# Sums and high parts ahead of a product's evacuation, low parts behind it, in a Strassen feed-forward

## The chip, the cores and the metric

The kernel runs on one core of a Trainium2 chip. The metric is device time of one execution in microseconds: 1438.63 us is the median of three runs (1437.92 to 1440.17). A single profiled execution took 1436.92 us, of which the trace covers a span of 1435.1 us from the first instruction to the last. All durations below come from that execution.

## What is computed

A decoder block over a sequence of 1024 positions and 1024 channels, in float32: adaLN-modulated RMS norm, a differential attention branch and a causal convolution branch with sigmoid gates, an output projection, and then a feed-forward part, which is what the change touches:

```
h2 = rmsnorm(x, norm2_g) * (1 + sc2) + sh2
fg, fu = split(h2 @ w_ffn_in)            # 1024 -> 2 x 2816
x = x + gt2 * ((silu(fg) * fu) @ w_ffn_out)   # 2816 -> 1024
return rmsnorm(x, final_g)
```

The 2816 hidden channels are 22 tiles of 128 (the gated tiles, numbered 0 to 21). Activations lie transposed: channels on partitions, positions along the free dimension.

## The kernel before

**Precision.** Every float32 matrix product is made of three matmuls. An operand is split into a high part (ScalarE, called ACT, writes a rounded copy, `split_hi`) and a low part (VectorE, called DVE, subtracts the high part from the source). The three matmuls are high by high, high by low, low by high.

**Strassen form.** Both halves of the feed-forward use a seven-product form of a 2 x 2 block product. A `Pair` (line 1150) covers two gated tiles of the gate matrix or of the up matrix: pair i works on tiles 2(i//2) and 2(i//2)+1, even i on the gate, odd i on the up side. There are 22 pairs of seven products, each product twelve matmuls of 128 x 512 (four blocks of the contraction, three matmuls each). The products of a pair go to three PSUM banks, X, Z, X, Z, X, Y, X (line 1152), so that the next product but one adds into the same bank. In between, `evacuate(p)` reads the bank out: after products 0, 1, 2 ACT copies it to `kepta`, `keptc`, `keptb`; after products 3, 4, 5 DVE adds the kept copy and ACT applies SiLU (gate), or DVE adds and multiplies with the gate (up); after product 6 one of them reads the bank. TensorE may add to a bank only when it has been read out.

**Weights.** `load` fetches the raw weights of pair i+2 at product 1 of pair i. `prepare` makes a weight block for a product: for some a DVE sum of raw blocks (`tt`), then the ACT high part, then the DVE low part. Blocks are made `LEAD` = 6 products ahead, in a turn of ten: six tiles `wb` and four `wbp`.

**Staging of the second half.** The gated tiles of nine up pairs (tiles 0 to 17) are the left operands of the output product, again in Strassen form. `g_steps` (line 1299) makes for each two tiles seven blocks (four of them with a DVE sum, all with an ACT high part and a DVE low part) and stores them to DRAM from GpSimd's queue (`gs_d`). The seven steps run one in a product, from product 4 of the up pair to product 3 of the next gate pair; for the first tiles two in a product. Tiles 18 to 21 are stored as they are (`g_d`), and are used at the end in the common form (three matmuls each, no sums).

**The output product.** `Group` (line 1267) covers two of the eight output tiles and three pairs of gated tiles: twelve groups of seven products of nine matmuls. Its blocks come back from `gs_d` (`gb`, GpSimd's queue). Its evacuation adds the bank on DVE to the residual tile `x1r`, which is loaded from DRAM on SP's queue (line 1474). Last come the four common tiles: their weights are loaded (line 1540) and their products added (from line 1570), then the final norm.

**Order.** In this stage TensorE, DVE and ACT issue in the program's order (`in_order`, line 1399), so one late instruction holds all behind it on its engine. The queues of SP and GpSimd have no such written order; the framework places their DMAs, and buffers are taken from shared pools: 32 slots of 128 x 1024 (`slot`), the `wb` pool of six, and small pools. The main loop is at line 1479; for each product it runs, in this order:

```
prepare(nprep)         # up to two: sum, high part, low part
g.product(p)           # TensorE
late.pop(0)()          # a staging step: sum, high, low, store
g.evacuate(p)
```

Of the kernel before, what the change touches and what calls it, by code (L numbers as in the profile page):

```python
# [10 lines left out]
F32 = mybir.dt.float32  # L11
F32R = mybir.dt.float32r
AF = mybir.ActivationFunctionType
ALU = mybir.AluOpType
AX = mybir.AxisListType

P = 128
S = 1024
D = 1024
KD = D // P  # L20
# [6 lines left out]
NFF = DFF // P  # L27
# [3 lines left out]
HB = 512  # L31
# [39 lines left out]
NWB = 10  # L71
LEAD = 6
LEAD2 = 4
NST = 9
GP = 3

GB = ("A11", "S1", "S2", "S4", "S3", "A12", "A22")
# [21 lines left out]
def tile_hybrid_block(ctx: ExitStack, tc: tile.TileContext, xT, vecs, cvec, lamv, relb, bsel, bmask, jrev,  # L99
                      w_ada, w_v, w_in, w_oa, w_oc, w_out, w_fi, w_fo, outT):  # L100
    nc = tc.nc
# [25 lines left out]
    V, A, T, G = Engine(nc.vector), Engine(nc.scalar), Engine(nc.tensor), nc.gpsimd  # L127
# [11 lines left out]
    def slot(name, dt=F32):  # L139
        return sp.tile([P, S], dt, tag="s4", name=name)  # L140

    def t2(name, dt=F32):
        return tp.tile([P, HB], dt, tag="t2", name=name)
# [10 lines left out]
    def hf_sl(hf):  # L154
        return slice(hf * HB, (hf + 1) * HB)

    def split_hi(dst, src, scale=1.0):
        return A.activation(dst, src, AF.Copy, scale=scale)

    def split(hi, lo, src):  # L160
        split_hi(hi, src)
        V.tensor_tensor(out=lo, in0=src, in1=hi.bitcast(F32), op=ALU.subtract)
# [7 lines left out]
    class Weights:  # L170
# [4 lines left out]
        def load(self):  # L175
            self.raw = wp.tile([P, D], F32, tag="wraw", name=f"wr_{self.name}")
            if len(self.src.shape) == 3:
                k = self.src.shape[0]
                nc.sync.dma_start(self.raw[:, :self.n].rearrange("p (a n) -> p a n", a=k),
                                  self.src.rearrange("a p n -> p a n"))  # L180
            else:
                nc.sync.dma_start(self.raw[:, :self.n], self.src)
# [19 lines left out]
    def mm3(out, sh, sl, mh, ml, start, stop, **kw):  # L202
        T.matmul(out, sh, mh, start=start, stop=False, **kw)
        T.matmul(out, sh, ml, start=False, stop=False, **kw)
        T.matmul(out, sl, mh, start=False, stop=stop, **kw)
# [114 lines left out]
    y = []  # L320
# [40 lines left out]
    def bankG(name):  # L361
        return psG.tile([P, HB], F32, tag="G", name=name)

    with tc.tile_pool(name="psS", bufs=2, space=bass.MemoryType.PSUM) as psS, \
# [253 lines left out]
        class Proj:  # L618
# [5 lines left out]
            def step(self, s):  # L624
                hf, k = divmod(s, KD)
                if s == 0:
                    self.out = self.begin()
                if k == 0:
                    self.ps = bankG("proj")
                ks = slice(k * P, (k + 1) * P)  # L630
                mm3(self.ps, self.w.hi[:, ks], self.w.lo[:, ks], hhi[k][:, hf_sl(hf)], hlo[k][:, hf_sl(hf)],
                    k == 0, k == KD - 1)
                if k == KD - 1:
                    self.evac(self.ps, self.out, hf)
# [185 lines left out]
        for h in range(H):  # L820
# [8 lines left out]
            sm, wf, tw, nm = {}, {}, {}, {}  # L829
# [63 lines left out]
    with tc.tile_pool(name="ps2", bufs=6, space=bass.MemoryType.PSUM) as ps2, ExitStack() as fxs:  # L893
# [112 lines left out]
        for m in range(0, KD, 2):  # L1006
            i = [j[1] for j in jobs].index(m + 1) + 1
# [29 lines left out]
        x1 = []  # L1037
# [59 lines left out]
        g_d = dp.tile([NFF, P, S], F32, name="g_d")  # L1097
        gs_d = dp.tile([NST * 7, P, S], F32R, name="gs_d")
        acts = {}
        fx, ada_last = [], []  # L1100
# [49 lines left out]
        class Pair:  # L1150
# [4 lines left out]
            n = HB  # L1155
# [34 lines left out]
            def prepare(self, p):  # L1190
                self.low(self.high(p))
# [69 lines left out]

            def store(self, n):
                f = self.f + n
                if self.up and f >= 2 * NST:
                    G.dma_start(g_d[f], hidden[f])

        class Group(Pair):

            n = GP * P
# [9 lines left out]
            def load(self):  # L1279
                b = []  # L1280
                for n in range(2):
                    raw = self.raw(self.up)
                    c0 = self.g * 2 * self.n
                    nc.sync.dma_start(raw[:, :2 * self.n], w_fo[self.m + n][:, c0:c0 + 2 * self.n])
                    t = raw[:, :2 * self.n].rearrange("p (a h n) -> p h a n", h=2, n=P)
                    b.append((t[:, 0], t[:, 1]))
                (b11, b21), (b12, b22) = b
                self.b = dict(B11=b11, B21=b21, B12=b12, B22=b22)
# [10 lines left out]
        def g_steps(i):  # L1299

            a11, a21 = (hidden[2 * i][:, hf_sl(hf)] for hf in range(2))
            a12, a22 = (hidden[2 * i + 1][:, hf_sl(hf)] for hf in range(2))

            def put(name, src):
                t = slot("gst", F32R)
                split(t[:, :HB], t[:, HB:], src)
                G.dma_start(gs_d[i * 7 + GB.index(name)], t)  # L1307

            def summed(name, out, x, y, op=ALU.subtract):
                def f():  # L1310
                    t = out if out is not None else t2("gs1")
                    V.tensor_tensor(out=t, in0=x, in1=y, op=op)
                    put(name, t)
                return f

            return [lambda: put("A12", a12), lambda: put("A22", a22), lambda: put("A11", a11),
                    summed("S1", None, a21, a22, ALU.add), summed("S3", a21, a11, a21), summed("S2", a11, a22, a21),
                    summed("S4", a12, a12, a11)]

        hidden = {}  # L1320
        pairs = [Pair(i) for i in range(NFF)]
# [1 line left out]
        order = [(pairs[j], p) for p in (0, 5, 1, 2, 3, 4, 6) for j in range(2)]  # L1323
        order += [(g, p) for g in pairs[2:] for p in range(7)]
        nblock, nfx = [0], [NWB - 4]
# [126 lines left out]
        nprep = 17  # L1452

        gacts = {}
        x1 = []
        ORDER = [a for a, b, x in Pair.PRODUCTS]
        wanted = [(g, name, k) for g in range(NST // GP) for name in ORDER for k in range(GP)]

# [13 lines left out]
        def x1r():  # L1472
            x1.append(slot(f"x1r{len(x1)}"))
            nc.sync.dma_start(x1[-1], x1_d[len(x1) - 1])

        seq = pairs + [Group(i) for i in range(NST // GP * KD // 2)]
        order += [(g, p) for g in seq[NFF:] for p in range(7)]
        late = g_steps(0)
        for n, (g, p) in enumerate(order):
            if n < 14:  # L1480
                continue
            i = n // 7
            first = i < NFF
            if p == (1 if first else 3) and i + 2 < len(seq):
                seq[i + 2].load()
            for _ in range(2):
                if nprep < len(order) and nprep <= n + (LEAD if nprep < 7 * NFF else LEAD2):
                    nfx[0] = NWB - 4 if nprep < 7 * NFF else 2
                    prepare(nprep)
                    nprep += 1  # L1490
            g.product(p)
            if first:
                if g.up and p == 4 and g.i // 2 < NST:
                    late = g_steps(g.i // 2)
                for _ in range(2 if n < 18 else 1):
                    if late:
                        late.pop(0)()
            g.evacuate(p)
            if first:
                if not g.up and p == 5 and ada_todo and g.i >= 4:  # L1500
                    (c, k), ch = ada_todo.pop(0), slot("ada2")
                    nc.sync.dma_start(ch, w_ada[c, k])
                    ada_last.append((c, k, ch))
                if g.up and p == 2 and ada_last:
                    ada_sum(*ada_last.pop(0))
                if i == NFF - 1:
                    fetch_blocks(0, GP)
                    if p >= 5:
                        x1r()
            else:  # L1510
                if i < NFF + 4 and len(x1) < KD:
                    x1r()
                if g.m == 2 and p == 0:
                    fetch_blocks(g.g + 1, 7)
                elif g.m == KD - 2:
                    fetch_blocks(g.g + 1, GP)
# [10 lines left out]
            split(hi, raw, raw.bitcast(F32))  # L1527
            return hi, raw

        grp = list(range(2 * NST, NFF))  # L1530
        n = len(grp)
        raws = [fetch(f) for f in grp]
        g_acts = [g_split(f, raw) for f, raw in zip(grp, raws)]
# [1 line left out]
        for q in range(0, KD, S // (n * P)):  # L1535
            nm = S // (n * P)
            lo = slot("fol", F32R)
            hi = slot("foh", F32R)
            raw = wp.tile([P, D], F32, tag="wraw", name="for")
            nc.sync.dma_start(raw.rearrange("p (m c) -> p m c", m=nm),  # L1540
                              w_fo[q:q + nm, :, grp[0] * P:(grp[0] + n) * P].rearrange("m p c -> p m c"))
            split(hi, lo, raw)
            for i in range(nm):
                wl.append((hi[:, i * n * P:(i + 1) * n * P], lo[:, i * n * P:(i + 1) * n * P]))

        parts = (slice(0, HB), slice(HB, HB + HB // 2), slice(HB + HB // 2, S))
        stf, accs, lasts, rest = {}, {}, {}, []
# [22 lines left out]
        for i, hs in enumerate(parts):  # L1570
# [3 lines left out]
            for m in range(KD):  # L1574
# [4 lines left out]
                t = x1[m][:, hs]  # L1579
# [83 lines left out]
```

## Time and profile before

| | |
|---|---|
| median of three runs | 1438.63 us |
| profiled execution | 1436.92 us |
| its span | 1435.1 us |
| TensorE matmul busy (PE) | 1350.5 us, 94% |
| weight loads of TensorE (PEld) | 1094.1 us, 76% |
| VectorE (DVE) | 1070.8 us, 75% |
| ScalarE (ACT) | 637.7 us, 44% |
| GpSimd (POOL) | 104.1 us, 7% |
| mean granted clock of TensorE | 0.985 of full |

Busy shares are means over stages with different limits. The feed-forward pairs run from about 710 us to 1191 us of the span, the output product's groups to 1374, the common tiles and the final norm to the end. Matmuls are pipelined and their ends are modelled, so the distance between the starts of two products is the safer measure than a busy share. An engine named as the releaser of a wait is the one that came last by the profile.

### The profile page before, as it was taken

What the parts mean: (1) busy time and instruction counts of PE and PEld (TensorE: products, weight loads), DVE (VectorE), ACT (ScalarE), POOL (GpSimd) and SP (SyncE); (2) the same over time, 40 slices, a digit from 0 to 9 for tenths busy, and PEclk for the clock granted to TensorE, in tenths of its full rate; (3) what the DMA queues carried; (4) which work ended last, traced back from release to release, by engine and by line L of the source; (5) the groups of instructions that cost most, each with busy time, mean ns of one, the idle gap of its engine ahead of it and who ended that gap; (6) DMA issues with size and microseconds to landing.
All of it is one profiled execution on the core that took longest, in us unless ns stands there. A gap on an engine that the chain in (4) does not pass through costs nothing. (4 is left out here: it accounts for less than half of the span.)

```text
span 1435.1 us, 16435 instructions
## 1 busy us (share of the span) xinstructions
PE 1350.5 (94%) x6070; PEld 1094.1 (76%) x6070; DVE 1070.8 (75%) x1698; ACT 637.7 (44%) x1079; POOL 104.1 (7%) x181
## 2 busy tenths in 40 slices
PE   7999999999999999999987999999999997999996
PEld 5778787877888887788765777777777786888886
DVE  7837698899988996976896666666766645777775
ACT  5536766666412117433764444444444431222255
POOL 0000000000000000000001000011000022112004
PEclk9999999999999999999999999999999998999998
DMA  8511011000111124278313443453443359587313
GB/s 312 168 35 40 30 30 30 30 30 31 45 53 50 44 89 132 88 262 309 103 59 123 141 146 125 154 175 134 153 152 136 132 198 385 192 302 264 110 30 118
DMA packets 57811, 184.43 MB, mean 129 GB/s; under 512 B 6361, under 2 KB 9345, under 8 KB 57730
## 3 DMA queue, kind: packets, MB, share of 16 engines
q1 hardware_dynamic: 37154, 110.49, 23.2%
q0 software_dynamic: 20000, 72.36, 14.0%
q8 instruction: 48, 0.79, 0.2%
q10 hardware_dynamic: 576, 0.52, 0.1%
q14 instruction: 33, 0.27, 0.1%
HBM read 139.83 MB, written 43.52 MB: 128 GB/s over the span
## 5 line engine op out<-in xcount | busy, mean ns | idle before, releaser
L112 DVE SCALAR_TENSOR_TENSOR cacc<-u,vec,cacc 128x1022 f32<-128x1022 f32 (+28 forms) x87 | 110.2, 1267 | 2.2
L112 PE MATMUL proj<-hhi,wh_in 128*128 128x512 f32 x239 | 99.3, 415 | 1.7 <-DVE kl L124 1.7
L112 ACT ACTIVATE wbp<-tt 128x512 fp32r<-128x512 f32 (+1 forms) x66 | 38.1, 579 | 131.3 <-DVE tt L112 110.8
L112 PE MATMUL proj<-hhi,wl_in 128*128 128x512 f32 x240 | 94.9, 395 | 0.0
L112 PE MATMUL proj<-hlo,wh_in 128*128 128x512 f32 x240 | 94.7, 394 | 0.0
L112 PE MATMUL fx<-A,wb 128*128 128x512 f32 x335 | 80.1, 393 | 13.0 <-DVE g L112 13.0
L112 PE MATMUL fx<-S,wb 128*128 128x512 f32 x312 | 76.6, 394 | 8.9 <-ACT keptb L112 5.0
L112 PEld LDWEIGHTS fx<-A,wb 128*128 128x128 f32 x335 | 62.3, 188 | 29.2 <-DVE g L112 12.7
L112 ACT ACTIVATE wb<-tt 128x512 fp32r<-128x512 f32 (+1 forms) x68 | 41.1, 606 | 94.3 <-DVE tt L112 77.9
L112 DVE TENSOR_TENSOR wb<-tt,wb 128x512 fp32r<-128x512 f32 (+1 forms) x68 | 44.7, 660 | 48.0 <-ACT wb L112 47.9
L112 PE MATMUL fz<-S,wb 128*128 128x512 f32 x312 | 76.1, 392 | 1.7 <-DVE S L112 1.6
L112 DVE TENSOR_TENSOR wbp<-tt,wbp 128x512 fp32r<-128x512 f32 (+1 forms) x66 | 41.3, 627 | 48.1 <-ACT wbp L112 48.1
L112 PEld LDWEIGHTS fx<-S,wb 128*128 128x128 f32 x312 | 57.7, 188 | 25.6 <-ACT keptb L112 7.1
L112 PEld LDWEIGHTS fz<-S,wb 128*128 128x128 f32 x312 | 58.0, 188 | 16.6 <-DVE S L112 2.4
L112 PE MATMUL fx<-gb,wbp 128*128 128x512 f32 x282 | 68.6, 390 | 0.1
L112 ACT ACTIVATE gst<-g 128x512 fp32r<-128x512 f32 x54 | 33.9, 629 | 69.1 <-DVE g L112 42.9
L112 PE MATMUL fx<-S,wbp 128*128 128x512 f32 x216 | 53.8, 396 | 8.2 <-ACT keptb L112 4.6
L112 PEld LDWEIGHTS fx<-gb,wbp 128*128 128x128 f32 x282 | 52.8, 188 | 11.5 <-DMA gb<-gs_d 0.5
L1307 POOL DMA_DIRECT2D gs_d<-gst x63 | 33.5, 532 | 382.5 <-DVE gst L112 382.5
L112 PE MATMUL fz<-S,wbp 128*128 128x512 f32 x216 | 55.2, 406 | 6.4 <-ACT keptc L112 4.9
L124 ACT ACTIVATE e<-sc,mn 128x512 f32<-128x512 f32 (+7 forms) x64 | 47.1, 739 | 25.9 <-DVE mn L124 25.0
L112 PEld LDWEIGHTS fx<-S,wbp 128*128 128x128 f32 x216 | 39.7, 188 | 21.4 <-ACT keptb L112 6.6
(347 smaller groups left out, 3610.4 us busy)
## 6 DMA issues: line engine op xcount, KB each, us to landing
gs_d<-gst POOLq DMA_DIRECT2D x63, 512.0 KB, 2.9
gb<-gs_d POOLq DMA_DIRECT2D x59, 512.0 KB, 9.4
ada<-in_w_ada SPq DMA_DIRECT2D x32, 512.0 KB, 4.3
rawu<-in_w_fi SPq DMA_DIRECT2D x22, 512.0 KB, 3.5
rawg<-in_w_fi SPq DMA_DIRECT2D x22, 512.0 KB, 3.6
adac<-in_w_ada SPq DMA_DIRECT2D x16, 512.0 KB, 5.3
wr_wo<-in_w_out SPq DMA_DIRECT2D x16, 512.0 KB, 5.0
wr_in<-in_w_in SPq DMA_DIRECT2D x15, 512.0 KB, 3.5
```

Of the source, the lines that this page charges most:

```text
L112: self.last = f(*args, **kw)
L124: self.last = self.chain(f, *args, **kw) if self.chain else f(*args, **kw)
L1307: G.dma_start(gs_d[i * 7 + GB.index(name)], t)
```

## The change

In the main loop the weight block and the staging step are cut in two: the sum and the high part are issued between a product and its evacuation, the low parts (and the staging block's store) behind the evacuation. One staging step runs in a product, never two. The lead is five products, and the turn of weight blocks eight (four `wb`, four `wbp`). Of the seven staging blocks of two tiles, three still take a slot and four take a tile of the `wb` pool. The Strassen form covers tiles 2 to 19; tiles 0, 1, 20 and 21 are in the common form, so that their weights are no longer contiguous and are loaded in two halves. The residual tiles are fetched at products 3 and 5 of the first groups (two in a group) instead of one in each product.

```diff
-NST = 9
+STR = range(1, 10)
+NST = len(STR)
...
-                if self.up and f >= 2 * NST:
+                if self.up and f // 2 not in STR:
                     G.dma_start(g_d[f], hidden[f])
...
-            def put(name, src):
-                t = slot("gst", F32R)
-                split(t[:, :HB], t[:, HB:], src)
-                G.dma_start(gs_d[i * 7 + GB.index(name)], t)
...
+            def step(name, src, x=None, y=None, op=ALU.subtract):
+
                 def f():
-                    t = out if out is not None else t2("gs1")
-                    V.tensor_tensor(out=t, in0=x, in1=y, op=op)
-                    put(name, t)
+                    t = src
+                    if x is not None:
+                        t = src if src is not None else t2("gs1")
+                        V.tensor_tensor(out=t, in0=x, in1=y, op=op)
+                    if name in ("A11", "S1", "S4"):
+                        b = slot("gst", F32R)
+                    else:
+                        b = fx[0].tile([P, D], F32R, tag="wb", name="gstw", bufs=NWB - 4)
+                    split_hi(b[:, :HB], t)
+
+                    def rest():
+                        V.tensor_tensor(out=b[:, HB:], in0=t, in1=b[:, :HB].bitcast(F32), op=ALU.subtract)
+                        G.dma_start(gs_d[(i - STR[0]) * 7 + GB.index(name)], b)
+                    return rest
                 return f
...
-        late = g_steps(0)
+        late = []
...
+            g.product(p)
+            if first and g.up and p == 4 and g.i // 2 in STR:
+                late = g_steps(g.i // 2)
+            lows = []
             for _ in range(2):
-                if nprep < len(order) and nprep <= n + (LEAD if nprep < 7 * NFF else LEAD2):
-                    nfx[0] = NWB - 4 if nprep < 7 * NFF else 2
-                    prepare(nprep)
+                if nprep < len(order) and nprep <= n + (LEAD if n < 16 else LEAD - 1 if nprep < 7 * NFF else LEAD2):
+                    nfx[0] = NWB - 6 if nprep < 7 * NFF else 2
+                    h = order[nprep][0]
+                    lows.append(partial(h.low, h.high(order[nprep][1])))
                     nprep += 1
-            g.product(p)
-            if first:
-                if g.up and p == 4 and g.i // 2 < NST:
-                    late = g_steps(g.i // 2)
-                for _ in range(2 if n < 18 else 1):
-                    if late:
-                        late.pop(0)()
+            if late:
+                lows.append(late.pop(0)())
             g.evacuate(p)
+            for f in lows:
+                f()
...
-                if i < NFF + 4 and len(x1) < KD:
+                if p in (3, 5) and len(x1) < KD:
                     x1r()
...
-        grp = list(range(2 * NST, NFF))
+        grp = [f for f in range(NFF) if f // 2 not in STR]
...
-            nc.sync.dma_start(raw.rearrange("p (m c) -> p m c", m=nm),
-                              w_fo[q:q + nm, :, grp[0] * P:(grp[0] + n) * P].rearrange("m p c -> p m c"))
+            for i in range(0, n, 2):
+                nc.sync.dma_start(raw.rearrange("p (m c) -> p m c", m=nm)[:, :, i * P:(i + 2) * P],
+                                  w_fo[q:q + nm, :, grp[i] * P:(grp[i] + 2) * P].rearrange("m p c -> p m c"))
```

## Rows read from the trace of the kernel before

**Rows 1.** The page: busy time, share of the span and instructions of each engine.
```profile
PE 1350.5 (94%) x6070; PEld 1094.1 (76%) x6070; DVE 1070.8 (75%) x1698; ACT 637.7 (44%) x1079; POOL 104.1 (7%) x181
```

**Rows 2.** Windows: length, busy us (instructions) by engine, granted clock, DMA share, GB/s.
```profile
765.00:796.00 31.00, 22.05 (x83) 16.59 (x82) 19.16 (x30) 13.45 (x24) 3.72 (x7) 0.89 0.49 170
...
924.00:966.00 42.00, 38.78 (x168) 30.80 (x167) 29.06 (x45) 17.47 (x32) 3.72 (x7) 1.00 0.44 150
...
1136.00:1191.00 55.00, 55.00 (x244) 45.56 (x243) 30.17 (x47) 18.14 (x32) 10.95 (x21) 1.00 0.55 185
1191.00:1214.00 23.00, 14.73 (x55) 11.65 (x54) 8.83 (x15) 2.64 (x6) 6.17 (x12) 0.78 1.07 389
```

**Rows 3.** Waits of TensorE, 764 to 1191: us in total, times, longest.
```profile
PE fx L112 <- DVE g L112: 15.3, 9, 1.7
PE fx L112 <- ACT keptb L112: 9.6, 9, 1.6
```

**Rows 4.** Timeline of TensorE, late pairs: start, us, instruction, [idle before <-releaser].
```profile
985.41 2.88 PE L112 MATMUL fz<-S,wb 128*128 128x512 f32 x12
988.77 3.01 PE L112 MATMUL fx<-S,wbp 128*128 128x512 f32 x12 [0.49 <-ACT kepta L112]
...
995.85 3.04 PE L112 MATMUL fx<-S,wbp 128*128 128x512 f32 x12 [1.01 <-ACT keptb L112]
...
1003.29 5.73 PE L112 MATMUL fx<-A,wb 128*128 128x512 f32 x24 [1.69 <-DVE g L112]
...
1136.46 2.88 PE L112 MATMUL fz<-S,wb 128*128 128x512 f32 x12
...
1190.86 2.20 PE L112 MATMUL fx<-gb,wbp 128*128 128x512 f32 x9
```

**Rows 5.** Timeline of TensorE, first gate pair.
```profile
764.61 2.88 PE L112 MATMUL fz<-S,wb 128*128 128x512 f32 x12
...
776.17 5.49 PE L112 MATMUL fz<-S,wbp 128*128 128x512 f32 x12 [4.86 <-ACT keptc L112]
...
796.26 2.88 PE L112 MATMUL fz<-S,wb 128*128 128x512 f32 x12
```

**Rows 6.** Timeline, a gate pair with staging: sums, low part, high part, read-out.
```profile
819.79 0.69 DVE L112 TENSOR_TENSOR g<-g 128x512 f32<-128x512 f32 x1
...
823.22 0.69 DVE L112 TENSOR_TENSOR wbp<-tt,wbp 128x512 fp32r<-128x512 f32 x1 [0.70 <-ACT wbp L112]
823.83 0.69 DVE L112 TENSOR_TENSOR g<-g,g 128x512 f32<-128x512 f32 x1
824.60 0.63 ACT L112 ACTIVATE gst<-g 128x512 fp32r<-128x512 f32 x1 [1.41 <-DVE g L112]
825.13 0.58 ACT L112 ACTIVATE keptb<-fx 128x512 f32<-128x512 f32 x1
```

**Rows 7.** Timeline at the change from pairs to groups.
```profile
1192.66 2.56 SPq L1474 DMA_DIRECT2D x1r<-x_d  x5
...
1202.51 0.75 DVE L112 SCALAR_TENSOR_TENSOR x1r<-fx,cols,x1r 128x512 f32<-128x512 f32 x1 [9.14 <-DMA x1r<-x_d]
...
1203.37 4.18 PE L112 MATMUL fx<-gb,wb 128*128 128x512 f32 x9 [8.27 <-issue]
...
1210.03 2.20 PE L112 MATMUL fx<-gb,wbp 128*128 128x512 f32 x9
```

**Rows 8.** The page: DMA issues, KB each, median us from issue to landing.
```profile
gs_d<-gst POOLq DMA_DIRECT2D x63, 512.0 KB, 2.9
```

**Rows 9.** Timeline at the start of the common tiles.
```profile
1373.94 0.39 PE L124 MATMUL fo<-gh,foh 128*128 128x512 f32 x1
...
1377.53 1.22 DVE L124 TENSOR_TENSOR fol<-for,foh 128x1024 fp32r<-128x1024 f32 x1
```

**Rows 10.** The tile x1r, 1185 to 1215: its loads to their landing.
```profile
DMA to landing us min/median/max: 11.7/13.6/15.7
```

**Rows 11.** Timeline of the first gate pair, ACT.
```profile
775.00 0.63 ACT L112 ACTIVATE gst<-gs 128x512 fp32r<-128x512 f32 x1 [3.08 <-DMA gs_d<-gst]
```

More of the change, by code (lines that the diff above doesn't have):

```diff
@@ L1282, in load @@
                     raw = self.raw(self.up)
-                    c0 = self.g * 2 * self.n
+                    c0 = 2 * P * STR[0] + self.g * 2 * self.n
                     nc.sync.dma_start(raw[:, :2 * self.n], w_fo[self.m + n][:, c0:c0 + 2 * self.n])
@@ L1302, in g_steps @@
             a12, a22 = (hidden[2 * i + 1][:, hf_sl(hf)] for hf in range(2))
-            def put(name, src):
-                t = slot("gst", F32R)
-                split(t[:, :HB], t[:, HB:], src)
-                G.dma_start(gs_d[i * 7 + GB.index(name)], t)
-            def summed(name, out, x, y, op=ALU.subtract):
-                def f():
-                    t = out if out is not None else t2("gs1")
-                    V.tensor_tensor(out=t, in0=x, in1=y, op=op)
-                    put(name, t)
-                return f
-            return [lambda: put("A12", a12), lambda: put("A22", a22), lambda: put("A11", a11),
-                    summed("S1", None, a21, a22, ALU.add), summed("S3", a21, a11, a21), summed("S2", a11, a22, a21),
-                    summed("S4", a12, a12, a11)]
+            def step(name, src, x=None, y=None, op=ALU.subtract):
+                def f():
+                    t = src
[11 more added lines that the diff above has]
+                    return rest
+                return f
+            return [step("A12", a12), step("A22", a22), step("A11", a11), step("S1", None, a21, a22, ALU.add),
+                    step("S3", a21, a11, a21), step("S2", a11, a22, a21), step("S4", a12, a12, a11)]
         hidden = {}
```

## The prediction

> **What bounds the kernel now.** I read the page first: TensorE has 1350.5 us of matmul in a span of 1435.1, DVE 1070.8, ScalarE (ACT) 637.7 [rows 1]. TensorE sets the time, so a change pays only where TensorE stands still. The windows say where that is. Through the steady part of the gated feed-forward (924 to 966 us) it is busy 38.78 of 42 us at full clock; from 1136 to 1191, with no staging steps left, 55.00 of 55; at the change to the output product (1191 to 1214) 14.73 of 23, at a granted clock of 0.78; in the first stretch (765 to 796) 22.05 of 31 at 0.89 [rows 2]. The waits of the feed-forward name one cause: TensorE waits for a PSUM bank to be read out, by DVE (15.3 us, nine times) or by ACT's copy keptb (9.6 us, nine times) [rows 3]. DMA and weights hardly appear there.
>
> The TensorE timeline gives the size. A product without a wait takes 2.72 us: the twenty from 1136.46 to 1190.86 take 54.40 [rows 4]. A period is one gate pair and one up pair, fourteen products, 38.08 us. The eight periods from 796.26 to 1136.46 take 340.20, so 42.53 each: 4.45 lost in each, 35.6 in all [rows 4, 5]. Inside a period the loss lies in the gate pair: 985.41 to 988.77 is 3.36 (0.64 too long), the next two products 7.08 (1.64), the next two 7.44 (2.00) [rows 4]. The first gate pair, with two staging steps in a product, takes 31.65 from 764.61 to 796.26 where seven products want 19.04: 12.6 lost, 4.86 of it in one wait for the copy keptc, after which twelve matmuls took 5.49 [rows 5]. Together 48.2 us.
>
> Why the read-out is late shows in ACT's and DVE's order. Each product's queue holds sum, high part (ACT), low part (DVE) of a weight block, the same three of a staging step, and only then the read-out. Every low part waits for its high part, so the two engines take turns: one staging sum starts at 819.79, the next at 823.83, 4.04 us apart against 2.72 of a product, and keptb comes at 825.13 behind the second step's high part of 824.60 [rows 6]. DVE is busy only 29.06 of 42 us there and ACT 17.47 [rows 2]: it is the order, not the amount.
>
> **The change, part by part.** *Low parts behind the read-out.* Per product DVE now holds weight sum, staging sum, (read-out), weight low, staging low; ACT holds weight high, staging high, read-out. Let TensorE end a product at E, with ACT's copy (0.58 us) as read-out [rows 6]. The copy is done near E+0.8; the bank's next writer starts at E+2.72, one product later, so 1.9 us are spare. ACT then makes the next product's two high parts (0.63 each, 0.53 apart as from 824.60 to 825.13) [rows 6] by E+2.0; their sums were issued ahead and are done. DVE's two lows (0.69, and 0.61 apart as from 823.22 to 823.83) [rows 6] end at E+2.75, its next two sums at E+3.4 and E+4.0, and the next highs are due at E+3.5 and E+4.05. So a product with everything in it holds 2.72. The tightest is the gate pair's fourth, where five DVE instructions fall together (two sums, the bank's read-out, two lows): 5 x 0.61 = 3.05, 0.33 over; the next has three (1.83) and pays it back. Work is unchanged: 29.06 us of DVE against 38.08 of a period.
>
> So the 35.6 us and the 12.6 us go. The first gate pair has no staging at all now, since the first two tiles leave the Strassen form. The last gate pair gets seven steps instead: 4.45 in the old order, nothing in the new by the same schedule. Bounds: nothing gained (0) to all 48.2. I take 1.5 back, 0.15 for each of ten gate pairs, for the tight fourth product: 46.7.
>
> *Lead of five, eight weight blocks in turn, four of seven staging blocks in the weight pool.* A low part for product n+5 is done about 2.75 us after product n, and is wanted three products later (8 us of cover); its block was last read by product n-3. At most four of the pool's six tiles then hold weights, two are left for staging, and a staging tile is free after its store lands (2.9 us) [rows 8], some two products on. I cost this at 0. If the cover fails, ACT stands at a high part with the read-out queued behind it and TensorE behind that (second rival).
>
> *Tiles 0, 1 for 18, 19.* The two stores of tiles 0 and 1 go out early, when the DMA engines are about half busy (0.49) [rows 2], two later ones disappear: 0. *Residual weights of the end in two halves.* Four loads become eight. The third one's low part runs at 1377.53, TensorE reaches its tile at 1373.94 + 4 x 2.72 = 1384.8 [rows 9]: about 6 us of cover, cost 0 (up to 2 if the halves land late).
>
> *Residual two tiles at a time.* At the change of stage TensorE loses 11.0 us: four products of nine matmuls want 8.16 and take 19.17 (1190.86 to 1210.03) [rows 4, 7]. DVE waited 9.14 us for the first residual tile, issued at 1192.66 in a run of five, and let TensorE go at 1203.37, where the granted clock was half for a while (4.18 us for nine matmuls, against 2.20 later) [rows 7]. In that window the engines are full: DMA share 1.07, 389 GB/s [rows 2]. Two tiles instead of five take 3 x 0.524 MB = 1.57 MB out of it, 4.0 us at that rate. That is the most it can give, since the staged blocks then come last and were loaded in the same window. The least is a loss: the later tiles stand behind another weight load on SP's queue, worked out below as about 2 us. I take +1.0.
>
> Here a page speaks against the change. The Trainium skill (page "DMA: Bandwidth & Descriptors", section "Queues, rings and completion order") says that an engine consumes a queue's descriptors in ring order and takes turns between queues packet by packet. Then tiles queued behind the first one on the same queue do not delay it, and the first tile comes no sooner. The trace has not shown either: all eight loads took 11.7 to 15.7 us, median 13.6 [rows 10]. By that rule the sum would be 1392 for the 1391 below.
>
> Sum: 1436.92 (the profiled execution; its span is 1435.1) - 46.7 - 1.0 = 1389.2. The median of the runs shown is 1.7 above that execution, so I forecast 1391 us.
>
> **Rivals.** *First tile no sooner, later ones late.* By a queue served in order the 11.0 us stay. The third residual tile, wanted by the second group's first read-out, is now issued at that group's predecessor's fourth product, near 1208, behind two weight loads; at 13.6 us it lands at 1221.6. The read-out is due at 1210.03 + 4 x 2.04 = 1218.2, so 3.4 late, less one product of slack (2.04), plus the read-out (0.75): 2.1 lost. Time 1391 + 1.0 + 2.1 = 1394. For it: the loads' 13.6 us [rows 10]. Against: less traffic by then.
>
> *The wait moves to the tiles.* A high part of a weight waits on ACT for a staging tile's store. It is free near E+2.75 + 0.5 (the issue) + 2.9 = E+6.2, wanted near E+3.5: 2.7 late, 0.8 beyond the spare 1.9. Four such tiles in each of nine periods: 29 us, so 1420. For it: two kinds of tile share six buffers, and which buffer follows which is settled at compile time. Against: the count above.
>
> *Slower.* In the first gate pair ACT stood 3.08 us at a staging high part for an earlier store, with the copy that TensorE waited 4.86 for behind it [rows 5, 11]; that pair lost 12.6 us. If every gate pair did so, nine of them lose 113.5, 65 more than now: 1504. It decides from 48.2 / 9 = 5.4 us lost in a pair. Against: it came with two steps in a product; the later pairs lost 4.45.
>
> *The change does nothing of note*: SP's loads are not in a written order, and the engines' order could be bound by something that the trace does not show: 1438.
>
> **How the numbers follow.** Forecast (1385 to 1392.9): 0.49. First rival (1393 to 1399): 0.25. Second (1400 to 1430): 0.16. Slower: 0.06. No change: 0.03. The whole 11 us of the stage change going too (1380): 0.01. The range 1385 to 1410 holds 0.49 + 0.25 and somewhat over a third of the second rival. Faster by over 0.2% (what a measurement can tell from no change): 0.91, within it 0.03, slower 0.06.
>
> **What would show it.** Right: a TensorE timeline with product starts 2.72 apart in the gate pairs too, no wait for kepta, keptb, keptc or g worth 2 us, DVE low parts starting after the bank's read-out, the period at 38.1. The second rival shows as ACT idle before a high part, ended by a DMA of the staging. The first shows as DVE waiting for a residual tile in the first group (about 9 us) and again in the second. The forecast is wrong if the period stays above 39 us.

## The result and the profile after

The changed kernel takes 1387.70 us, the median of four runs (1385.42 to 1389.20), where the kernel before took 1439.18 (1437.92 to 1440.17) beside it. The ratio is 0.9641, with a 95% interval of 0.9625 to 0.9658. The profiled execution took 1385.42 us, and its span is 51.5 us shorter. From the page, beside [rows 1]:

```profile
span 1383.6 us, 16481 instructions
...
PE 1333.2 (96%) x6070; PEld 1091.0 (79%) x6070; DVE 1067.0 (77%) x1698; ACT 636.8 (46%) x1079; POOL 104.1 (8%) x181
```

The engines' instruction counts are those of before, and the busy times of DVE and ACT differ by less than 4 us, so no work was taken out. TensorE's windows, with the columns of [rows 2], show where the 51.5 us were. The fourth line is one whole period of fourteen products.

```profile
763.00:796.00 33.00, 33.00 (x147) 27.35 (x146) 19.79 (x32) 14.76 (x27) 0.00 (x0) 1.00 0.22 75
924.00:966.00 42.00, 42.00 (x187) 34.79 (x186) 32.14 (x51) 19.96 (x35) 4.25 (x8) 1.00 0.50 161
1141.00:1164.00 23.00, 14.84 (x60) 11.87 (x59) 9.85 (x17) 3.24 (x7) 6.17 (x12) 0.85 1.08 395
896.27:934.35 38.08, 38.08 (x169) 31.53 (x168) 28.62 (x45) 17.87 (x31) 3.72 (x7) 1.00 0.52 166
```

In these windows of the pairs TensorE is busy all the time. At the change to the output product it is busy 14.84 of 23 us, as before. The wait list of TensorE from 757 to 1165 (us in total, times, longest) has one row where [rows 3] had two long ones; it lies at that change:

```profile
PE fx L113 <- issue: 8.2, 1, 8.2
```

The TensorE timeline answers to [rows 4, 5]. Every product in between starts 2.72 us behind the one ahead of it:

```profile
762.99 2.88 PE L113 MATMUL fz<-S,wb 128*128 128x512 f32 x12
...
934.35 2.88 PE L113 MATMUL fz<-S,wbp 128*128 128x512 f32 x12
937.07 2.88 PE L113 MATMUL fx<-S,wbp 128*128 128x512 f32 x12
...
1141.07 2.20 PE L113 MATMUL fx<-gb,wbp 128*128 128x512 f32 x9
```

I take the **pair stage** from product 1 of the first gate pair to the first product of the groups (products count from 0; the first gate pair is the one behind the two opening pairs, which run interleaved): before 764.61 to 1190.86, 426.25 us [rows 4, 5]; after 762.99 to 1141.07, 378.08 us, which is 139 products of 2.72. So 48.17 us of the 51.5 are here. The length is steady: five executions give the same 378.08 (this one and four of the experiments, which ran on three chips). The four products at the change take 18.01 us (1141.07 to 1159.08, below) against 19.17 [rows 7], another 1.16. Of the rest, 1.62 us is the pair stage starting earlier; the first product of all pairs is already as much earlier (708.55 for 710.17), ahead of anything that was changed.

The timeline of a gate pair with staging shows the new order on DVE and ACT, against [rows 6]:

```profile
877.21 0.69 DVE L113 TENSOR_TENSOR gs<-g,g 128x512 f32<-128x512 f32 x1
...
877.93 0.63 ACT L113 ACTIVATE gst<-gs 128x512 fp32r<-128x512 f32 x1 [0.92 <-DVE gs L113]
878.47 0.58 ACT L113 ACTIVATE kepta<-fx 128x512 f32<-128x512 f32 x1
878.59 0.69 DVE L113 TENSOR_TENSOR gst<-gs,gst 128x512 fp32r<-128x512 f32 x1
...
879.80 0.68 DVE L113 TENSOR_TENSOR g<-g 128x512 f32<-128x512 f32 x1
```

ACT's copy kepta follows the high part at once and waits for no low part; the low part runs beside it. The two staging sums shown are 2.59 us apart, where two were 4.04 [rows 6].

### The profile page after: what moved, and what is told of

The parts are those of the page before. It is cut to its first block, busy times and chain, and to the rows that moved or that the text cites. A ratio compares the mean times of both kernels' runs of the same rounds, so it can differ in the third digit from the quotient of the medians.

```text
span 1383.6 us, 16481 instructions
## 1 busy us (share of the span) xinstructions
PE 1333.2 (96%) x6070; PEld 1091.0 (79%) x6070; DVE 1067.0 (77%) x1698; ACT 636.8 (46%) x1079; POOL 104.1 (8%) x181
## 4 chain that ended last, share of the span: by engine, by line
PE 68%; issue 11%; DVE 9%; ACT 6%; DMA 5%; POOL 1%; SPq 0%; DVEq 0%; ACTq 0%; POOLq 0%
PE fx L113 19%; PE fz L113 9%; PE proj L113 8%; PE ga L113 5%; PE fy L113 5%; PE gc L113 4%; PE oa L113 3%; PE oc L125 3%; DMA ada<-in_w_ada 3%; PE wo L125 3%; PE sc L113 2%; PE vacc L125 2%; PE av L113 2%; DMA gb<-gs_d 1%; DMA xs<-in_xT 1%
## 5 line engine op out<-in xcount | busy, mean ns | idle before, releaser
L113 PE MATMUL fx<-S,wbp 128*128 128x512 f32 x276 | 67.1, 391 | 1.4 <-DVE S L113 1.3
L113 PE MATMUL fz<-S,wbp 128*128 128x512 f32 x276 | 66.5, 390 | 1.5 <-ACT S L113 1.3
L113 PE MATMUL fz<-S,wb 128*128 128x512 f32 x252 | 61.0, 390 | 1.6 <-DVE S L113 1.6
L113 PEld LDWEIGHTS fx<-S,wbp 128*128 128x128 f32 x276 | 51.6, 188 | 13.5 <-DVE S L113 2.5
L113 PE MATMUL fx<-S,wb 128*128 128x512 f32 x252 | 60.8, 390 | 1.4 <-DVE S L113 1.3
L113 PEld LDWEIGHTS fz<-S,wbp 128*128 128x128 f32 x276 | 51.7, 188 | 12.9 <-ACT S L113 1.7
L113 DVE SCALAR_TENSOR_TENSOR x1r<-fx,cols,x1r 128x512 f32<-128x512 f32 x48 | 36.0, 751 | 30.6 <-PE fx L113 20.8
L113 PEld LDWEIGHTS fz<-S,wb 128*128 128x128 f32 x252 | 47.1, 188 | 12.1 <-DVE S L113 2.4
L113 PEld LDWEIGHTS fx<-S,wb 128*128 128x128 f32 x252 | 47.2, 188 | 11.9 <-DVE S L113 1.6
L113 DVE TENSOR_TENSOR wbp<-tt,wbp 128x512 fp32r<-128x512 f32 (+1 forms) x75 | 47.1, 629 | 11.7 <-ACT wbp L113 11.6
L113 PEld LDWEIGHTS proj<-hhi,wh_in 128*128 128x128 f32 x239 | 45.0, 188 | 11.1 <-issue 3.6
## 6 DMA issues: line engine op xcount, KB each, us to landing
gb<-gs_d POOLq DMA_DIRECT2D x59, 512.0 KB, 10.3
```

Of the source, the lines that this page charges most:

```text
L113: self.last = f(*args, **kw)
```

## The experiments

All were run beside the kernel before on the same chip (its medians: 1437.60 beside the first four below; 1437.99 beside the last two and the one with all seven blocks in slots; 1436.26 beside the other four). Ratios are against that. The pair stage of each trace is worked out as above.

**The order alone.** The kernel before, with high parts ahead of the evacuation and low parts behind it, and a staging block's store behind its low part; nothing else of the change.

```diff
+            g.product(p)
+            lows = []
...
-                    prepare(nprep)
+                    h = order[nprep][0]
+                    lows.append(partial(h.low, h.high(order[nprep][1])))
...
-            g.product(p)
...
-                        late.pop(0)()
+                        lows.append(late.pop(0)())
             g.evacuate(p)
+            for f in lows:
+                f()
```

> The kernel before with one part of the change: sums and high parts ahead of a product's read-out, low parts behind it. Lead 6, ten weight blocks in turn, all seven staging blocks in slots, tiles 0 to 17 in the Strassen form and the residual as before. Theory (the order makes TensorE wait): the eight periods fall from 42.5 to 38.1 us each, 35.6 us; the first gate pair, which still has two steps in a product, keeps 3 to 9 of its 12.6; so 1396 to 1402 for 1439, and no wait of TensorE for kepta, keptb or g after the first gate pair. Rival (the order needs the other buffers too, since a staging slot is now held through the read-out): ACT stands at staging high parts for a store to land, and less than 20 us are gained.

1406.85 us, ratio 0.9782 (0.9755 to 0.9809): 30.8 us of gain. The pair stage is 394.51 us, 31.7 of the 48.2:

```profile
763.47 2.88 PE L112 MATMUL fz<-S,wb 128*128 128x512 f32 x12
...
788.62 2.88 PE L112 MATMUL fz<-S,wb 128*128 128x512 f32 x12
...
1157.98 2.20 PE L112 MATMUL fx<-gb,wbp 128*128 128x512 f32 x9
```

That is less than my theory said and more than the rival, but the rival's mechanism is there. Of the 16.4 us still lost, 6.1 are in the first gate pair with its two steps in a product (25.15 us for 19.04), 10.3 in the other eight. The waits of TensorE and then of ACT (740 to 1195) show what is behind it; the last row is the same wait of ACT in the kernel before (764 to 1191):

```profile
PE fz L112 <- ACT keptc L112: 5.5, 7, 3.1
PE fx L112 <- ACT kepta L112: 3.0, 8, 0.8
```

```profile
ACT gst L112 <- DMA gs_d<-gst: 32.9, 21, 2.6
```

```profile
ACT gst L112 <- DMA gs_d<-gst: 3.6, 2, 3.1
```

TensorE still waits for ACT's copies, and ACT stands 21 times at a staging high part until an earlier store has landed. In the kernel before it stood there twice, in the first gate pair, and with the common tiles alone (below) its list has no such wait; so with these buffers the new order brings the waits. It holds a staging slot longer (the low part and the store come behind the read-out) and uses the slots faster; no run separates the two. In the changed kernel ACT has no such wait in the pairs.

**The old order alone put back.** The changed kernel with all its buffers and tiles, but sum, high and low of a block together ahead of the evacuation.

```diff
-            g.product(p)
...
-                    lows.append(partial(h.low, h.high(order[nprep][1])))
+                    h.low(h.high(order[nprep][1]))
...
+            g.product(p)
...
-                lows.append(late.pop(0)())
+                late.pop(0)()()
```

> The changed kernel with the order alone put back: sum, high part, low part and store ahead of the read-out; its lead, buffers, common tiles and residual stay. Theory: each of the nine gate pairs with staging loses 4.45 us again, 40 us, so 1428 for 1388. Rival (buffers or lead did it): within 10 us of the changed kernel.

1424.99 us, 0.9907 (0.9882 to 0.9932). The pair stage is 416.76 us, 38.7 more than after, 4.30 for each of nine gate pairs. Its two ends, and the longest waits of TensorE from 757 to 1182, of the kind in [rows 3] again:

```profile
764.06 2.88 PE L113 MATMUL fz<-S,wb 128*128 128x512 f32 x12
...
1180.82 2.20 PE L113 MATMUL fx<-gb,wbp 128*128 128x512 f32 x9
```

```profile
PE fx L113 <- DVE g L113: 15.5, 9, 1.7
```

**The residual fetched as before.** The changed kernel, one residual tile at each product.

```diff
-                if p in (3, 5) and len(x1) < KD:
+                if i < NFF + 4 and len(x1) < KD:
```

> The changed kernel with the residual tiles fetched one in a product again. SP's queue had put them in runs of four and four in the changed kernel, of five and three in the one before; here five and three again. If two tiles a time was worth the 1.0 us forecast, 1389 for 1388 and the first group's third product starts later; if a tile behind the first in the same queue costs the first nothing, the same time within 1 us, and the first residual tile still lands about 9 us after it was issued.

1391.19 us, 0.967 (0.9646 to 0.9694); its pair stage is 378.08. The timelines at the change of stage, this kernel and then the changed one:

```profile
1146.10 2.20 PE L113 MATMUL fx<-gb,wbp 128*128 128x512 f32 x9
...
1148.41 2.48 SPq L1481 DMA_DIRECT2D x1r<-x_d  x5
...
1158.55 4.06 PE L113 MATMUL fx<-gb,wb 128*128 128x512 f32 x9 [8.21 <-issue]
...
1164.51 2.20 PE L113 MATMUL fx<-gb,wbp 128*128 128x512 f32 x9
```

```profile
1141.07 2.20 PE L113 MATMUL fx<-gb,wbp 128*128 128x512 f32 x9
...
1143.38 1.89 SPq L1481 DMA_DIRECT2D x1r<-x_d  x4
...
1152.62 0.75 DVE L113 SCALAR_TENSOR_TENSOR x1r<-fx,cols,x1r 128x512 f32<-128x512 f32 x1 [9.73 <-DMA x1r<-x_d]
1153.48 3.72 PE L113 MATMUL fx<-gb,wb 128*128 128x512 f32 x9 [8.16 <-issue]
...
1157.67 1.82 SPq L1481 DMA_DIRECT2D x1r<-x_d  x4
...
1159.08 2.20 PE L113 MATMUL fx<-gb,wbp 128*128 128x512 f32 x9
...
1167.24 1.07 PE L113 MATMUL fz<-gb,wb 128*128 128x512 f32 x4
```

The program's "two at a time" leaves SP's queue as four and four; "one at a time" leaves it as five and three. The wait is 8.16 or 8.21 us. The four products take 18.41 here; over the kernels with the old fetch they take 18.17 (order alone) to 19.65 (common tiles alone), with the new one 18.01 to 19.57 (lead, turn and staging buffers as before, below). The ranges lie over each other, and so do the intervals of this ratio and of the changed kernel's (0.9625 to 0.9658).

**The common tiles alone.** The kernel before, with tiles 0, 1, 20 and 21 in the common form and the weights of the end in halves.

```diff
+STR = range(1, 10)
+NST = len(STR)
...
-        late = g_steps(0)
+        late = []
...
-        grp = list(range(2 * NST, NFF))
+        grp = [f for f in range(NFF) if f // 2 not in STR]
```

> The kernel before with tiles 0, 1, 20, 21 in the common form and nothing else: the old order, one step in a product after each of nine up pairs. Theory: the first gate pair's 12.6 us go, the last gate pair's 4.45 come: 8.2 us less, 1431 for 1439. Rival (what the first gate pair lost was the start of the stage and not its staging steps): 4 us more than before.

1429.21 us, 0.994 (0.9919 to 0.9961), 8.4 less than before (5.6 to 11.6 by the interval), as worked out. The first gate pair takes 19.74 us where it took 31.65 [rows 5]. Its timeline:

```profile
769.74 2.88 PE L113 MATMUL fz<-S,wb 128*128 128x512 f32 x12
...
789.48 2.88 PE L113 MATMUL fz<-S,wb 128*128 128x512 f32 x12
```

The last gate pair has steps now, so the pair stage is only 7.63 less: 418.62 (769.74 to 1188.36).

**More work on DVE, in the new order.** The changed kernel, with each weight's low part in the pairs made twice.

```diff
             for f in lows:
                 f()
+                if first and f.__class__ is partial:
+                    f()
```

> The changed kernel with every weight block's low part in the pair stage computed twice (the second instruction writes the same values again): 14 more DVE instructions in a period, at 0.61 us 8.5 us. Theory (order, not amount): DVE then works about 40 of the 38.1 us of a period with its waits for ACT, so it is just the bound; a period becomes 39 to 41 us, 1400 to 1415 in all for 1388, still under the 1439 of the kernel before, which did a fifth less on DVE. Rival (DVE's amount was what the kernel before lacked): the 8.5 us come back in full in each period, 76 us and more, 1465.

1414.93 us, 0.9849 (0.9833 to 0.9865). The pair stage is 403.06 us (764.41 to 1167.47), 2.78 more for each of nine gate pairs. A window of about one period, and the longest waits of TensorE in the pairs:

```profile
1000.00:1040.80 40.80, 38.95 (x169) 31.25 (x168) 37.62 (x60) 17.66 (x32) 3.73 (x7) 1.00 0.48 155
```

```profile
PE fx L113 <- ACT kepta L113: 15.4, 9, 1.7
```

DVE is busy 37.62 of 40.8 us, nine us more than in the changed kernel's period of 38.08, and the kernel is still 21 us faster than the one before, whose DVE had 29.06 of 42 [rows 2].

**Lead, turn and staging buffers as before.** The changed kernel with a lead of six, ten weight blocks in turn and every staging block in a slot.

```diff
-                    if name in ("A11", "S1", "S4"):
-                        b = slot("gst", F32R)
-                    else:
-                        b = fx[0].tile([P, D], F32R, tag="wb", name="gstw", bufs=NWB - 4)
+                    b = slot("gst", F32R)
...
-                if nprep < len(order) and nprep <= n + (LEAD if n < 16 else LEAD - 1 if nprep < 7 * NFF else LEAD2):
-                    nfx[0] = NWB - 6 if nprep < 7 * NFF else 2
+                if nprep < len(order) and nprep <= n + (LEAD if nprep < 7 * NFF else LEAD2):
+                    nfx[0] = NWB - 4 if nprep < 7 * NFF else 2
```

> The changed kernel with the buffers of before: lead 6, ten weight blocks in turn, all seven staging blocks in slots. The order alone left 1.0 to 1.2 us lost in a period, with ACT waiting 21 times for a staging slot's store. If the new buffers remove that, they are worth 9 x 1.1 = 10 us here: 1398 for 1388, with ACT waits for gs_d stores again. Forecast's view (buffers cost and bring nothing): 1388.

1399.13 us, 0.9736 (0.9713 to 0.9759). The pair stage is 388.45 us (765.74 to 1154.19), 10.4 more than after. This run did not say which of the three edits did it, so two more took them apart.

**All seven staging blocks in the weight pool.**

```diff
-                    if name in ("A11", "S1", "S4"):
+                    if False:
```

> The changed kernel with all seven staging blocks in the pool of six weight tiles, none in slots: the prediction's second rival brought about. With seven staging and seven weight tiles in a period on six buffers, a high part on ACT waits for a staging store; at 0.8 us each, by the rival's arithmetic, four to seven a period: 4 to 5 us a period, 1425 to 1435. If two buffers are enough for a staging block in every product (each free about two products later), 1388 to 1392.

1392.04 us, 0.9692 (0.967 to 0.9715). The pair stage is 382.72 us (765.84 to 1148.56). Two buffers for staging are nearly enough. ACT's wait list has the stores again, but TensorE loses no more than 4.6 us:

```profile
ACT gstw L113 <- DMA gs_d<-gstw: 11.4, 5, 3.9
```

Of the 4.6, 3.8 are one wait and what follows it. The timeline of TensorE there, twelve matmuls that take 2.88 us elsewhere, at a granted clock of 0.58 (922.97 to 927 us):

```profile
922.97 4.61 PE L113 MATMUL fx<-S,wb 128*128 128x512 f32 x12 [1.93 <-ACT kepta L113]
```

**All seven in slots**, with the lead and the turn of the changed kernel. The edit is the first half of that under "Lead, turn and staging buffers as before".

> The changed kernel with all seven staging blocks in slots, its lead of five and eight weight blocks in turn kept. If the slots are what made ACT wait for stores (33.9 us, 20 times, with the old buffers), the waits and 10 us come back: 1398. If the lead or the turn of ten did it, 1388 and no such waits.

1400.42 us, 0.9736 (0.9717 to 0.9755). The pair stage is 388.83 us (765.72 to 1154.55), 10.75 more than after and within 0.4 us of that with all three put back: it is the slots, not the lead or the turn. ACT's wait list (800 to 1145), and its timeline at one of them:

```profile
ACT gst L113 <- DMA gs_d<-gst: 35.7, 18, 2.9
```

```profile
923.05 0.63 ACT L113 ACTIVATE gst<-gs 128x512 fp32r<-128x512 f32 x1 [2.13 <-DMA gs_d<-gst]
923.59 0.58 ACT L113 ACTIVATE kepta<-fx 128x512 f32<-128x512 f32 x1
...
924.22 3.04 PE L113 MATMUL fx<-S,wb 128*128 128x512 f32 x12
```

The high part waits 2.13 us for a store, the copy stands behind it, and TensorE starts as the copy ends (2.99 us behind the product ahead, 0.27 too long). ACT stands 35.7 us and TensorE loses 10.75: in the wait shown all but 0.27 us fits into the time that the copy has to spare.

**The first two residual tiles ahead of the blocks.** The changed kernel, with these two loads at products 0 and 1 of the last pair.

```diff
-                    fetch_blocks(0, GP)
-                    if p >= 5:
+                    if p < 2:
                         x1r()
+                    fetch_blocks(0, GP)
```

> The changed kernel with the first two residual tiles fetched at products 0 and 1 of the last pair, ahead of the staged blocks of those products, not at products 5 and 6 behind them. If the first tile's late landing is what holds TensorE 8.3 us at the first group, that wait goes; next late are the staged blocks of the group's last product: 9 blocks and two stores issued from 1138 on at 1.25 us each end near 1156, wanted at 1154, so about 2 us stay: 1379 for 1388. Rival (the window's transfers are the bound, whichever comes first): the wait moves to the staged blocks in full, 1387.

1386.31 us, 0.966 (0.9637 to 0.9682). I had expected 1379; the rival was right, and by the ratio this kernel is no faster than the changed one (0.9641). The timeline of the first group, from the slowest of its four executions (1391.52 us):

```profile
1148.69 2.20 PE L113 MATMUL fx<-gb,wbp 128*128 128x512 f32 x9
...
1160.47 0.97 PE L113 MATMUL fy<-gb,wbp 128*128 128x512 f32 x3 [0.74 <-DMA gb<-gs_d]
1163.03 0.96 PE L113 MATMUL fy<-gb,wbp 128*128 128x512 f32 x3 [1.59 <-DMA gb<-gs_d]
1167.44 6.39 PE L113 MATMUL fx<-gb,wbp 128*128 128x512 f32 x18 [3.45 <-DMA gb<-gs_d]
1173.67 1.53 PE L113 MATMUL fz<-gb,wb 128*128 128x512 f32 x6
```

The wait for the residual is gone, and TensorE waits for the staged blocks gb instead. To the second group's product 1 it takes 24.98 us, where eight products of 2.04 are 16.32: 8.66 lost (5.8 of it waits for gb, 2.2 slow matmuls in the row of eighteen, which take 4.24 us elsewhere), against 9.85 in the changed kernel (1141.07 to 1167.24).

**The stores of tiles 20 and 21 later as well**, written behind the first group's sixth product.

```diff
+                    if f < 2:
+                        G.dma_start(g_d[f], hidden[f])
+                    else:
+                        held.append(f)
...
+                if i == NFF and p == 5:
+                    for f in held:
+                        G.dma_start(g_d[f], hidden[f])
```

> The changed kernel with the first two residual tiles ahead of the staged blocks, as in the run before, and the stores of tiles 20 and 21 behind the first group's sixth product instead of ahead of its last nine blocks. With the residual first, TensorE waited 6.3 us for the blocks of the first group's last two products. Two stores of 0.52 MB at about 0.4 MB a microsecond leave that window, 2.6 us, and GpSimd's queue no longer stands at the first of them: 2 to 4 us less wait, so 8.7 lost in the first group becomes 5 to 7, and 1383 to 1385 where the changed kernel has 1388. Rival (the blocks' own 11 MB bound the window): no change from the run before, 1386.

1386.35 us, 0.9631 (0.9607 to 0.9656). The same stretch takes 23.40 us (1145.77 to 1169.17), 7.08 lost, still to gb:

```profile
PE fx L113 <- DMA gb<-gs_d: 3.3, 2, 1.7
```

The waits for gb are 3.8 us in all, where they were 5.8. The time is that of the rival, the stretch nearly the 5 to 7 expected. But the two stores did not leave the stretch. GpSimd's queue issued them behind all of the first group's blocks, yet 5.6 and 7.4 us after the group's start, and TensorE waited for blocks after that:

```profile
1151.36 0.54 POOL L1526 DMA_DIRECT2D g_d<-g  x1 [0.74 <-DMA gb<-gs_d]
1153.16 0.54 POOL L1526 DMA_DIRECT2D g_d<-g  x1 [1.27 <-DVE x1r L113]
```

**The changed kernel again**, on the chip of the run before and of the one with all seven in slots.

> The changed kernel as it is, on the same chip as the two others: 1385 to 1391, every pair product 2.72 us apart, 18 to 20 us for the first four products of the first group.

1389.72 us, 0.9658 (0.9638 to 0.9678); pair stage 378.08, and 26.57 us for the stretch (1145.02 to 1171.59). Beside it, the residual first with the later stores is 3.2 us better in this stretch of the trace and 3.4 by the medians, but the two intervals overlap: whether that version beats the changed kernel is not settled by time.

## Why the prediction was right, and where its steps were not

The forecast was 1391 us and the median is 1387.70, inside the range. What bounds the kernel was named rightly; which part of the change brings how much was not.

**The steps that held.** What bounded the kernel was the order: with it put back 38.7 of the 48.2 us return, though every buffer and tile is as after. The gate pairs run at 2.72 us a product, as the schedule said. The common tiles gave 8.4 us by themselves (8.2 worked out; 7.6 in the pair stage). Their stores and the weights' halves cost nothing: from 1300 us to the end of the common tiles TensorE waits for neither. The last gate pair's steps cost nothing in the new order. With nine us more of DVE in each period a read-out is late again, and even so the order wins: the amount of work was not the cause before.

**The 1.5 us for the tight fourth product** was too much: nothing was lost there.

**"Lead of five, eight weight blocks, four staging blocks in the weight pool: I cost this at 0"** is the term that was mis-sized. It costs nothing, but it is worth something: the sum counts the whole 48.2 for the order and the common tiles, and the order needs the buffers to get there. In the pair stage, one edit added to the others:

| kernel | pair stage, us | step |
|---|---|---|
| before | 426.25 | |
| order alone | 394.51 | -31.7 |
| and the common tiles, the lead, the turn and the fetch (all staging in slots) | 388.83 | -5.7 |
| after (four of seven staging blocks in the weight pool) | 378.08 | -10.75 |

The parts do not add up in another order: the common tiles alone are worth 7.6, and with the old order the rest of the change brings 1.9 more (418.62 to 416.76). The second rival, ACT held at a tile by its store, named the right mechanism and the wrong place. I looked for it in the new, shared pool and priced it at 29 us. It sits in the slots, at 10.75 us, and the pool is what takes it away. In the kernel before it stood only in the first gate pair [rows 11], 3.6 us in two waits; the new order makes it 21 waits, a price of the order that the sum left out. With all seven blocks in the pool it returns with 11.4 us of ACT and 4.6 of TensorE, 1.7 of these (4.61 less 2.88) by slower matmuls behind the one wait. That the sum still came out right is luck in part: the order's price and the buffers' worth cancel, because both are in the change.

**"Residual two tiles at a time: +1.0"** came out at 1.16 in the profiled execution, for a reason of its own, so its size was luck. The queue's first run was four tiles for five, not two, so 0.524 MB left the window and not 1.57; at 389 GB/s that is 1.3 us. What came is 0.10: the first tile was used 11.55 us after the group's start, where it had been 11.65 [rows 7], and the wait was 8.16 for 8.27. Two tiles for five at this place was never run. The rest of the 1.16 is the clock: the matmuls behind the wait run at the 1.2 GHz level for a while (granted clock 0.50 from 1153 to 1155 us, before from 1203 to 1207), shorter this time (3.72 us for nine, against 4.18). The same fetch gave 18.01 and 18.41 for the same four products in two executions, so this part of the change is worth nothing that these runs can tell.

The Trainium skill (page "DMA: Bandwidth & Descriptors", section "Queues, rings and completion order") says that an engine consumes a queue's descriptors in ring order. It would follow that tiles behind the first on its queue do not delay it, and the trace agrees, for one tile fewer: 11.55 for 11.65 us. By that rule the sum was 1392 us; it is too near the forecast of 1391 for the times to choose between them.

So the first half of the first rival, a first tile no sooner, held. Its other half, late tiles in the second group, did not come. It supposed that the program's place is the queue's place. The third tile went out in the first run of four, which the queue issued from 1143.38 us, 2.3 us after the group's start; the prediction had it 17 us after it (1208 less 1190.86). Nothing waited for it.

**The rest.** The sum for a profiled execution was 1389.2 us, and this one took 1385.42: 1.5 is the allowance, 1.6 that it reached the pair stage earlier, 0.2 the change of stage, and 0.5 lies behind it. The 1.6 lies ahead of the change and is chance, and this was the quickest execution of its four.

At the change of stage the residual is not the only thing late. DMA is full there (share 1.08, 395 GB/s), and with the residual out of the way TensorE waits for the staged blocks, 8.66 us lost for 9.85. That points to the bytes of the window as the bound, but no run shows it: none took the bytes out, and GpSimd's queue, in which blocks and stores stand in line, is the rival left.

## What to carry to other kernels

Where two in-order engines hand a block back and forth, issue the read-out that the bottleneck engine waits for behind the first half of the hand-over and ahead of the second; the busy shares need not change for it to pay. Then look at what else stands in that queue: a step that waits for a store's buffer holds the read-out as an engine would, and giving it buffers was worth 10.75 us here once the order was right; in the old order these waits were 3.6 us of ACT in all. A DMA's place in the program is not its place in its queue, so read the queue's own rows before a load is costed as earlier or later.

## What the runs showed of the hardware

A wait of one length can cost TensorE its length or twice that. The last products of the two opening pairs begin with a wait of 2.8 to 2.9 us for a DVE read-out in every one of these kernels, the kernel before included. They and the product behind them are 36 matmuls; here they are in the changed kernel's two profiled executions:

```profile
754.71 8.44 PE L113 MATMUL fx<-A,wb 128*128 128x512 f32 x36 [2.84 <-DVE g L113]
```

```profile
755.84 11.27 PE L113 MATMUL fx<-A,wb 128*128 128x512 f32 x36 [2.85 <-DVE g L113]
```

In the windows from 749 to 766 us the granted clock is 1.00 in the first and 0.80 in the second:

```profile
749.00:766.00 17.00, 14.16 (x63) 11.43 (x62) 13.16 (x22) 9.09 (x17) 1.07 (x2) 1.00 0.23 85
```

```profile
749.00:766.00 17.00, 14.15 (x50) 11.15 (x49) 10.91 (x18) 6.52 (x12) 1.06 (x2) 0.80 0.20 81
```

In the second the clock stood at the 1.2 GHz level for part of these matmuls after the wait (granted clock 0.50 from 756 to 760 us), which cost another 2.8 us (11.27 less 8.44). The other kernels of this study show 8.4 to 11.3 for the same row. So a difference of 3 us between two traces can be this alone, and a wait that is removed may have cost more than its length.
